# Part of the first layer's output projection into its attention, one table of score halves for both layers, and a last projection chunk by chunk

## The chip, the core and the metric

The kernel runs on 1 core of one Trainium2 chip. The metric is the device time of one execution in microseconds (us); lower is better. Three runs of the kernel before gave 2385.03, 2386.05 and 2387.29 us, median 2386.05. The engines are TensorE (PE in the profile; its weight loads are PEld), VectorE (DVE), ScalarE (ACT), GpSimd (POOL) and SyncE (SP), which issues nearly all DMAs here.

## What is computed

Two layers of a hybrid mixer over 1280 tokens: 1024 latent tokens (`NL`) and 256 context tokens (`NP`). They are the columns, and 1024 features are 8 tiles of 128 partitions. One layer, cut to what matters:

```
h = rmsnorm(x) * (1 + scale) + shift              # modulation of the layer
q, k, v, g_attn, hyena parts, lru parts = h @ w_in
y_attn = softmax(q k^T / 8) v                     # 8 heads, latent tokens also see 512 cached keys
y_hy   = x0 * long_conv(x1 * hv, filter)          # by FFT
y_lru  = rg_lru forward + backward                # the recurrent branch
mix = concat(y_attn * silu(g_attn), y_hy * silu(g_hy), y_lru * silu(g_lru))    # 12 tiles of 128 rows
x_new = x + gate * (mix @ w_out)                  # the output projection
```

After the second layer comes a final rmsnorm. Every operand of a matmul is split into two float16 halves, `hi` (rounded) and `lo` (the rest), and three products are added (hi hi, hi lo, lo hi), so one 128-row tile of a projection costs 3 matmuls for each chunk of columns. The chunks are `CH`: 512, 512 and 256 columns.

## The kernel before

**Order of a layer.** The input projections run tile by tile, with the recurrent branch and the FFT work woven between them; the gated hyena and recurrent outputs are split into halves and parked in DRAM (`park`, tensor `Md`, 8 tiles: 0 to 3 hyena, 4 to 7 recurrent). Then comes `attention`, then `outproj`. In the first layer `weave` lets two side streams run along with `outproj`: the filter spectra of the second layer (`fs`) and its modulation (`mod`, which is `ada_pairs`: 48 blocks of `w_ada` of 256 KB, each loaded, split by ScalarE and VectorE, and used by a pair of small matmuls, L505 and L506). The buffers of `ada_pairs` are the four of tag `bn`. The scheduler of the framework sets the final order of each engine's instructions from the order of emission.

**Attention.** There are 40 units (4 head pairs, 5 blocks of 256 queries, 2 heads). For each, `scores` makes the scores of 2 key tiles at a time in PSUM (L1201, L1202), takes the exponential on ScalarE, and splits it: `SPLIT` says for each of the 6 steps of a unit who makes `hi` (A: ScalarE, from PSUM once more; V: VectorE, a cast; G: GpSimd) and who subtracts for `lo` (V or G). The first layer had a table of its own, with a second row for the last head pair; per latent unit of the first three pairs it gives ScalarE 4 of 6 `hi`, VectorE 1 and GpSimd 1, and of the last pair ScalarE 1 and VectorE 5. The second layer's gives ScalarE all 6, and VectorE 2 of 6 subtractions. Between the score steps, `tick` runs the maxima of the next pairs (L1174 on TensorE, reduced at L1175 on VectorE). `values` multiplies with v (L1228, L1229), `emit_out` transposes (L1240) and gates.

**The output projection** adds, per output tile d and chunk, 12 mixer tiles in PSUM (`out_acc`, L1321), then `stt(x, acc, gt_t, xi)` on VectorE makes gate times acc plus the residual xi, which was loaded, and `Squares` gathers the squares for the next norm. The second layer (`l in SOON`) did a part of it early: `soon` is a side stream of `attention`; 24 steps, each of which loads xi, adds the 8 parked tiles (24 matmuls), applies gate and residual and stores the partial sum to `Xp` in DRAM. From unit 4 on, 0.71 steps go with each unit. Its `outproj` then adds only the four attention tiles to what it loads from `Xp`. For this the parked tiles are read back (`fetch`) ahead of the attention; in the first layer this came after it.

**End.** `outproj` takes the output tiles one by one, all three chunks of each, and only the last `LAST` = 2 together, chunk by chunk; behind a chunk's last tile come its norm (`rstd`) and `through`, which in the second layer scales and stores the result. The weights are split by `split_w` (L157 on ScalarE, L151 on VectorE) and held by `Weights` in 10 slots; a weight tile of 512 columns takes one.

## Time and profile before

| | |
|---|---|
| three runs, median | 2386.05 us (2385.03 to 2387.29) |
| the profiled execution | 2387.67 us, of which the span is 2385.9 |
| TensorE busy | 2107.8 us, 88% of the span, mean granted clock 0.959 |
| VectorE, ScalarE, GpSimd busy | 1812.1, 1226.4, 835.3 us (76, 51, 35%) |
| DMA | 215.62 MB, mean 90 GB/s |

The profile is of one execution. Shares of the span are means over stages with different limits, so the stages are read one by one. The span begins at 0; the first attention lies at 811 to 1095 us, the first output projection at 1095 to 1349, the second attention at 1973 to 2315 and the second projection with the end at 2315 to 2386. TensorE's clock stands as the share of full speed that was granted.

### The profile page before, as it was taken

How to read it: one execution, taken by the hardware profiler on the slowest of the kernel's cores; microseconds unless marked ns; L12 is line 12 of the kernel's file. 1: busy time of each engine (PE TensorE's matmuls, PEld its weight loads, DVE VectorE, ACT ScalarE, POOL GpSimd, SP SyncE). 2: the span in 40 equal slices, each digit the busy share in tenths (PEclk: the TensorE clock that was granted, in tenths of full speed). 3: DMA queues.
4: the chain of work that ended last, by engine and by line, in shares of the span. 5: the costliest groups of instructions: out<-in, count | busy, mean ns of one | idle time of the engine just before them, and what ended most of it. 6: DMA issues, size and time to landing. Idle time of an engine off the chain costs nothing. (4 is left out here: it accounts for less than half of the span.)

```text
span 2385.9 us, 38028 instructions
## 1 busy us (share of the span) xinstructions
PE 2107.8 (88%) x14288; PEld 1246.9 (52%) x14288; DVE 1812.1 (76%) x2888; ACT 1226.4 (51%) x2132; POOL 835.3 (35%) x762
## 2 busy tenths in 40 slices
PE   8777868989998888879998898999899898999996
PEld 2334434555555566665444444455555555666663
DVE  6987888487669899986868776766774998767546
ACT  6765754334333466654353577644333326656662
POOL 4442252124312467852202221131340316445440
PEclk9889989999999999979999999999999999999998
DMA  7315224134214410003563213122422334112114
GB/s 265 121 42 127 59 67 128 57 110 135 79 57 132 150 48 2 7 1 116 158 195 123 93 31 55 51 74 78 141 85 71 107 103 145 54 58 60 41 51 139
DMA packets 147786, 215.62 MB, mean 90 GB/s; under 512 B 21381, under 2 KB 71726, under 8 KB 147601
## 3 DMA queue, kind: packets, MB, share of 16 engines
q1 hardware_dynamic: 147600, 213.18, 30.0%
q8 instruction: 112, 1.84, 0.3%
q14 instruction: 74, 0.60, 0.1%
HBM read 165.49 MB, written 43.79 MB: 88 GB/s over the span
## 5 line engine op out<-in xcount | busy, mean ns | idle before, releaser
L685 PE MATMUL acc<-h,wh 128*128 128x512 f16 (+1 forms) x3264 | 865.1, 351 | 34.6 <-DVE f L151 14.3
L685 PE MATMUL acc<-h,wl 128*128 128x512 f16 (+1 forms) x1632 | 572.5, 351 | 0.0
L685 PEld LDWEIGHTS <-wh 128*128 128x128 f16 x3264 | 324.4, 100 | 319.8 <-issue 74.8
L154 POOL TENSOR_TENSOR y<-by,y 128x512 f16<-128x512 f32 x264 | 319.7, 1227 | 211.1 <-issue 93.7
L685 PEld LDWEIGHTS <-wl 128*128 128x128 f16 x1632 | 162.5, 100 | 160.5 <-issue 34.4
L157 ACT ACTIVATE f<-acc 128x512 f32<-128x512 f32 (+1 forms) x204 | 105.0, 519 | 248.6 <-PE acc L685 247.2
L157 ACT ACTIVATE by<-s 128x512 f32<-128x512 f32 x208 | 131.1, 631 | 154.4 <-PE s L1202 140.4
L1321 PE MATMUL acc<-h,wh 128*128 128x512 f16 (+1 forms) x768 | 203.6, 348 | 0.0
L151 DVE SCALAR_TENSOR_TENSOR a<-f,pr,a 128x1024 f32<-128x1024 f32 (+1 forms) x144 | 147.9, 1047 | 60.2 <-ACT a L157 57.4
L1175 DVE TENSOR_REDUCE mxl<-m 128x1 f32<-128x512 f32 x288 | 188.0, 680 | 7.2 <-PE m L1174 7.0
L1228 PE MATMUL o<-va,y 128*128 128x130 f16 x1600 | 166.8, 224 | 2.0 <-DVE f L151 1.6
L1229 PE MATMUL o<-va,y 128*128 128x65 f16 x1600 | 161.6, 195 | 5.1 <-POOL y L154 4.7
L154 DVE TENSOR_TENSOR y<-by,y 128x512 f16<-128x512 f32 x136 | 137.1, 1017 | 34.6 <-ACT y L157 34.2
L1229 PEld LDWEIGHTS <-y 128*128 128x128 f16 x1600 | 144.7, 99 | 34.0 <-issue 18.4
L157 ACT ACTIVATE wh<-wr 128x512 f16<-128x512 f32 x184 | 113.5, 625 | 93.8 <-PE acc L685 55.7
L1321 PEld LDWEIGHTS <-wh 128*128 128x128 f16 x1152 | 109.7, 98 | 95.0 <-issue 19.5
L1228 PEld LDWEIGHTS <-y 128*128 128x128 f16 x1600 | 146.6, 99 | 21.0 <-issue 14.4
L372 PE MATMUL m<-y,ld 128*128 128x256 f16 x960 | 127.4, 279 | 28.2 <-ACT y L157 10.8
L1174 PE MATMUL m<-k,a 128*128 128x512 f16 x288 | 110.7, 387 | 37.3 <-DVE mxl L1175 35.8
L154 DVE TENSOR_TENSOR y<-y,y 128x256 f32<-128x256 f32 (+4 forms) x160 | 129.8, 841 | 13.8 <-ACT y L157 13.7
L151 DVE SCALAR_TENSOR_TENSOR wl<-wr,wh 128x512 f16<-128x512 f32 x168 | 129.8, 785 | 11.4 <-ACT wh L157 10.4
L1321 PE MATMUL acc<-h,wl 128*128 128x512 f16 (+1 forms) x384 | 133.6, 348 | 0.0
(217 smaller groups left out, 4233.1 us busy)
## 6 DMA issues: line engine op xcount, KB each, us to landing
wr<-in_w_in SPq DMA_DIRECT2D x136, 256.0 KB
bn<-in_w_ada SPq DMA_DIRECT2D x64, 256.0 KB
wr<-in_w_out SPq DMA_DIRECT2D x48, 256.0 KB
ld<-in_fhl SPq DMA_DIRECT2D x56, 192.0 KB
h<-Md SPq DMA_DIRECT2D x16, 640.0 KB
h<-in_w_ada SPq DMA_DIRECT2D x16, 512.0 KB
Md<-ba SPq DMA_DIRECT2D x32, 256.0 KB
Hl<-by SPq DMA_DIRECT2D x32, 256.0 KB
```

The lines of the kernel that those rows point to most:

```text
L151: return (eng or V).scalar_tensor_tensor(out, a, s, b, o0, o1)
L154: (eng or V).tensor_tensor(out, a, b, op)
L157: A.activation(out, a, f, bias=bias, scale=scale)
L372: PE.matmul(x[:, o], cn[:, y, c], hl[:, z, g], start=(k == 0 and j == 0), stop=(k == 1 and j == 2))
L685: PE.matmul(acc[:, :n], w[k // 4][wi][:, P * (k % 4):P * (k % 4) + P], h[k][:, x, c0:c0 + n], start=(k == 0 and j == 0), stop=(k == KT - 1 ...
L1174: PE.matmul(p, lhs, k1[g][:, 512 * c:512 * c + 512], start=True, stop=True)
L1175: V.tensor_reduce(mxl[:, 8 * e + qt, c:c + 1], p, AX.X, MAX)
L1228: PE.matmul(o[:, qt], p[:, 0], va[g][:, s0 + s], start=(s == 0), stop=False)
L1229: PE.matmul(o[:, qt, 0], p[:, 1], va[g][:, s0 + s, 0], start=False, stop=(s == ns - 1))
L1321: PE.matmul(acc[:, :n], wt[:, cs], mix[k][:, x, c0:c0 + n], start=(i == 0 and j == 0), stop=(i == len(ks) - 1 and j == 2))
```

## The change

Three things are changed. (1) The side stream `soon` now runs in the first layer too, but over the four recurrent tiles alone (group 2 of the mixer tiles; `SOON` names for each layer the groups that go early): 24 steps of 12 matmuls. Weight tiles of a projection are now `u` (early) and `r` (rest) in both layers. The first `outproj` adds the other 8 tiles to the partial sums that it loads from `Xp`, and `fetch` comes ahead of the attention. (2) The second layer's row of `SPLIT` serves both layers. (3) `LAST` becomes 8 for the second layer: all its output tiles go chunk by chunk.

```diff
-N_G, LAST = (4, 4), 2
+N_G, LAST = (4, 4), (2, 8)
...
-SOON, SOON_RATE, SOON_FROM = (1,), 0.71, 4
-
-SPLIT = (("AG", "VV", "AG", "AV", "GG", "AG"), ("VG", "VG", "VV", "VV", "VV", "AG")), \
-    (("AG", "AG", "AV", "AG", "AG", "AV"), ("AG", "AG", "AV", "AG", "AG", "AV"))
+SOON, SOON_RATE, SOON_FROM = ((2,), (1, 2)), 0.71, 4
+
+SPLIT = "AG", "AG", "AV", "AG", "AG", "AV"
...
+    def groups(l, part):
+
+        return [i for i in (1, 2, 0) if (i in SOON[l]) == (part == "u")]
+
+    def tiles_of(l, part):
+        return [4 * i + j for i in groups(l, part) for j in range(4)]
...
-            how = SPLIT[l][last][s2 // 2]
+            how = SPLIT[s2 // 2]
...
-                acc = out_acc(w, [None] * 4 + parked, range(4, NMIX), c0, n)
+                acc = out_acc(w, [None] * 4 + parked, tiles_of(l, "u"), c0, n)
...
-        for ds in [(d,) for d in range(KT - LAST)] + [tuple(range(KT - LAST, KT))]:
+        for ds in [(d,) for d in range(KT - LAST[l])] + [tuple(range(KT - LAST[l], KT))]:
...
-                    xi = B("ld" if l in SOON else "ba")[:, :n]
-                    load(xi, (Xp if l in SOON else xT if l == 0 else Xs)[d, :, c0:c0 + n])
-                    acc = out_acc(w, mix, range(4) if l in SOON else [*range(4, NMIX), *range(4)], c0, n)
+                    xi = B("ld" if l else "ba")[:, :n]
+                    load(xi, Xp[d, :, c0:c0 + n])
+                    acc = out_acc(w, mix, tiles_of(l, "r"), c0, n)
...
-        if l in SOON:
-            drain(fill)
-            fetch()
-            mix = attention(l, h, st, gates, fill, EVERY[l], soon(l, parked))
-        else:
-            mix = attention(l, h, st, gates, fill, EVERY[l])
-            fetch()
-            mix += parked
+        drain(fill)
+        fetch()
+        mix = attention(l, h, st, gates, fill, EVERY[l], soon(l, parked)) + parked
```

The lines of the changed kernel are 1 lower above its new functions and 3 higher below them (L154 becomes L153, L1175 becomes L1178).

How this moves the instructions is seen best at three places, all on VectorE. The first is in the middle of the first attention (`mxl` are the maxima, `y` the halves of the exponentials, `by` the exponentials, `ba` the outputs, `ld` the stream's residual). Before:

```order
L1175 TENSOR_REDUCE mxl_7163<-m_8037 128x1
L154 TENSOR_TENSOR ba_7704<-ba_7704,o_7973 128x2x64
L1175 TENSOR_REDUCE mxl_7163<-m_8049 128x1
L154 TENSOR_TENSOR ba_7704<-ba_7704,ri_8022 128x2x64
L1214 CAST y_8032<-by_8045 128x512
L1175 TENSOR_REDUCE mxl_7163<-m_8062 128x1
L154 TENSOR_TENSOR y_8032<-by_8045,y_8032 128x512
L154 TENSOR_TENSOR y_8057<-by_8070,y_8057 128x512
```

And in the change:

```order
L1178 TENSOR_REDUCE mxl_7185<-m_8155 128x1
L1188 TENSOR_REDUCE mm_7186<-mxl_7185 128x16
L153 TENSOR_TENSOR y_8138<-by_8151,y_8138 128x512
L1235 RECIPROCAL ri_8207<-o_8158 128x2
L1236 COPY ba_8028<-o_8158 128x2x64
L153 TENSOR_TENSOR ba_8028<-ba_8028,o_8158 128x2x64
L153 TENSOR_TENSOR ba_8028<-ba_8028,ri_8207 128x2x64
L150 SCALAR_TENSOR_TENSOR f_6348<-o_8212,f_6348 128x256
L150 SCALAR_TENSOR_TENSOR ld_8218<-acc_8220,gt_t,ld_8218 128x256
```

The casts are gone, and the gated additions of the stream (`ld<-acc,gt_t,ld`) have come in; on TensorE 288 matmuls of the projection stand between the scores, in 24 groups of 12.

The second place is late in the first output projection, where the last of the modulation's six tables is copied out of PSUM (`bn<-s`). Before, 14 of the projection's 24 accumulations stand ahead of it:

```order
L151 SCALAR_TENSOR_TENSOR bn_12785<-bn_12784,bn_12785 128x512
L154 TENSOR_TENSOR by_11591<-by_11591,bn_12832 128x512
L510 TENSOR_SCALAR bn_12881<-s_12734 4x512
L154 TENSOR_TENSOR by_11592<-by_11592,bn_12931 128x512
L154 TENSOR_TENSOR modv<-s_12883,pr 128x8
L154 TENSOR_TENSOR by_11593<-by_11593,bn_13063 128x256
```

In the change 20 of 24 do; `a_13818` belongs to the last two output tiles:

```order
L150 SCALAR_TENSOR_TENSOR a_13818<-acc_13896,gt_t,ba_13894 128x512
L150 SCALAR_TENSOR_TENSOR bn_13121<-bn_13120,bn_13121 128x512
L153 TENSOR_TENSOR by_12053<-by_12053,bn_13156 128x512
L150 SCALAR_TENSOR_TENSOR y_13561<-y_13560,y_13304 128x256
L509 TENSOR_SCALAR bn_13205<-s_13070 4x512
L153 TENSOR_TENSOR by_12054<-by_12054,bn_13243 128x512
```

So the modulation's work now reaches nearly to the end of the projection's. Behind its last pair TensorE has 72 matmuls of the projection and 96 of the spectra, which stand in one block between the last two accumulations.

The third place is the end of the second projection (`fin_t` marks the final scaling, `acc` an accumulation). Before, the first chunk's scaling stands behind all long accumulations:

```order
L151 SCALAR_TENSOR_TENSOR a_25205<-acc_25275,gt_t,ld_25273 128x512
L154 TENSOR_TENSOR bn_25249<-bn_25249,bn_25247 128x512
L151 SCALAR_TENSOR_TENSOR a_25204<-acc_25320,gt_t,ld_25318 128x256
L151 SCALAR_TENSOR_TENSOR bn_25246<-bn_25249,bn_25247 128x512
L154 TENSOR_TENSOR by_24860<-by_24860,bn_25270 128x512
L151 SCALAR_TENSOR_TENSOR f_24862<-f_24862,fin_t,bn_25246 128x512
```

In the change it stands between those of the second chunk:

```order
L150 SCALAR_TENSOR_TENSOR bn_25142<-bn_25145,bn_25143 128x512
L153 TENSOR_TENSOR by_24980<-by_24980,bn_25183 128x512
L150 SCALAR_TENSOR_TENSOR f_24982<-f_24982,fin_t,bn_25142 128x512
L150 SCALAR_TENSOR_TENSOR f_24984<-acc_25188,gt_t,ld_25186 128x512
L150 SCALAR_TENSOR_TENSOR f_24983<-f_24983,fin_t,bn_25142 128x512
L150 SCALAR_TENSOR_TENSOR f_24984<-f_24984,fin_t,bn_25142 128x512
```

The 8 accumulations of the third chunk (256 columns), which before stood tile by tile among the others, now stand together at the end.

## Rows read from the trace of the kernel before

**Rows 1.** The page, part 1: busy time, share of the span, instructions.

```profile
PE 2107.8 (88%) x14288; PEld 1246.9 (52%) x14288; DVE 1812.1 (76%) x2888; ACT 1226.4 (51%) x2132; POOL 835.3 (35%) x762
```

**Rows 2.** Windows of three stages: us; PE, PEld, DVE, ACT, POOL busy; PEclk; DMA share, GB/s.

```profile
811.00:1095.00 284.00, 232.19 (x2621) 181.58 (x2619) 259.35 (x482) 167.29 (x334) 200.46 (x177) 0.93 0.12 37
1095.00:1349.00 254.00, 237.03 (x1298) 118.70 (x1298) 182.66 (x279) 114.17 (x195) 39.44 (x23) 0.98 0.49 154
1973.00:2315.00 342.00, 318.96 (x3204) 227.50 (x3202) 232.73 (x450) 219.96 (x443) 179.95 (x161) 0.99 0.22 67
```

**Rows 3.** Groups, first attention, PE: count | busy us, mean ns | idle before, releaser.

```profile
L1174 PE MATMUL m<-k,a 128*128 128x512 f16 x144 | 55.1, 387 | 27.1 <-DVE mxl L1175 26.4
```

**Rows 4.** Groups, second attention, PE.

```profile
L1321 PE MATMUL acc<-h,wh 128*128 128x512 f16 (+1 forms) x384 | 98.8, 343 | 0.0
...
L1321 PE MATMUL acc<-h,wl 128*128 128x512 f16 (+1 forms) x192 | 66.0, 344 | 0.0
L1174 PE MATMUL m<-k,a 128*128 128x512 f16 x144 | 55.6, 386 | 10.2 <-DVE mxl L1175 9.4
```

**Rows 5.** Groups, first attention, DVE: subtractions and casts.

```profile
L154 DVE TENSOR_TENSOR y<-by,y 128x512 f16<-128x512 f32 x72 | 75.9, 1071 | 0.3
L1214 DVE CAST y<-by 128x512 f16<-128x512 f32 x66 | 50.2, 781 | 4.3 <-ACT by L157 4.3
```

**Rows 6.** Groups, second attention, DVE: subtractions, the stream's additions, weight splits.

```profile
L154 DVE TENSOR_TENSOR y<-by,y 128x512 f16<-128x512 f32 x64 | 61.2, 957 | 34.3 <-ACT y L157 34.2
...
L151 DVE SCALAR_TENSOR_TENSOR ld<-acc,gt_t,ld 128x512 f32<-128x512 f32 (+1 forms) x24 | 15.9, 661 | 48.0 <-PE acc L1321 47.7
...
L151 DVE SCALAR_TENSOR_TENSOR wl<-wr,wh 128x512 f16<-128x512 f32 x16 | 11.0, 686 | 2.1 <-ACT wh L157 1.7
```

**Rows 7.** Groups, second attention, ACT: a rounded half from PSUM.

```profile
L157 ACT ACTIVATE y<-s 128x512 f16<-128x512 f32 x104 | 67.2, 646 | 0.0
```

**Rows 8.** Timeline, PE, end of the second projection: start us, us, instruction.

```profile
2357.07 0.38 PE L1321 MATMUL acc<-a,wl 128*128 128x512 f16 x1
...
2359.66 0.38 PE L1321 MATMUL acc<-a,wl 128*128 128x512 f16 x1
2359.87 0.38 PE L1321 MATMUL acc<-a,wh 128*128 128x256 f16 x2
2360.09 0.27 PE L1321 MATMUL acc<-a,wl 128*128 128x256 f16 x1
```

**Rows 9.** Windows: last head pair of the second attention and of the first.

```profile
2240.00:2315.00 75.00, 72.12 (x783) 54.21 (x780) 35.28 (x75) 53.55 (x109) 43.35 (x40) 1.00 0.14 44
1023.00:1095.00 72.00, 58.80 (x633) 47.67 (x632) 64.47 (x115) 33.07 (x63) 38.29 (x32) 0.80 0.03 9
```

**Rows 10.** Line L1321, second attention: ns min/median/max, first and last start.

```profile
L1321 PEld LDWEIGHTS <-wh x407: 95/98/98, 2014.0 to 2314.6; 128*128 128x128 f16 x136
```

**Rows 11.** Groups, first projection, DVE: weight splits.

```profile
L151 DVE SCALAR_TENSOR_TENSOR wl<-wr,wh 128x512 f16<-128x512 f32 x21 | 18.7, 900 | 0.3 <-PE acc L1321 0.2
```

**Rows 12.** Line L506, first projection: the second matmul of each modulation pair.

```profile
L506 PE MATMUL s<-bn,silu_p x48: 376/377/584, 1098.3 to 1274.4; 128*2 128x512 f16 x48
```

**Rows 13.** Waits, first projection: us in total, times, longest us.

```profile
ACT bn L157 <- DMA bn<-in_w_ada: 39.9, 23, 6.3
...
PE s L506 <- DVE bn L151: 7.7, 6, 3.8
```

**Rows 14.** Window from TensorE's last matmul of the projection to the end.

```profile
2362.40:2386.00 23.60, 2.60 (x7) 0.80 (x4) 19.30 (x33) 4.08 (x8) 2.83 (x3) 0.58 0.61 223
```

**Rows 15.** Timeline, DVE, the end: scaling, accumulation and addition of squares.

```profile
2363.15 0.74 DVE L151 SCALAR_TENSOR_TENSOR f<-f,fin_t,bn 128x512 f32<-128x512 f32 x1
2363.82 0.68 DVE L154 TENSOR_TENSOR by<-by,bn 128x512 f32<-128x512 f32 x1
...
2371.20 0.48 DVE L151 SCALAR_TENSOR_TENSOR a<-acc,gt_t,ld 128x256 f32<-128x256 f32 x1
...
2372.25 0.42 DVE L154 TENSOR_TENSOR by<-by,bn 128x256 f32<-128x256 f32 x1
```

More of the change, by code (lines that the diff above doesn't have):

```diff
@@ L647, in __init__ @@
                 names += [f"ga{i}" for i in range(4)]
-                names += [f"{x}{d}" for x in "ur" for d in range(KT)] if l in SOON else list(range(KT))
+                names += [f"{x}{d}" for x in "ur" for d in range(KT)]
                 self.todo += [(l, n) for n in names]
@@ L654, in pull @@
                 l, n = self.todo[0]
-                size = 3 if isinstance(n, int) else 1 if n[0] == "r" else 2
+                size = len(groups(l, n[0])) if n[0] in "ur" else 2
                 if need not in self.done and need is not None:
@@ L661, in pull @@
                 self.live.append(((l, n), size))
-                if isinstance(n, int):
-                    v = [split_w(w_out[l, n, :, 512 * i:512 * i + 512], WENG["o"]) for i in (1, 2, 0)]
-                elif n[0] in "ur":
-                    v = [split_w(w_out[l, int(n[1]), :, 512 * i:512 * i + 512], WENG["o"])
-                         for i in ((1, 2) if n[0] == "u" else (0,))]
+                if n[0] in "ur":
+                    v = [split_w(w_out[l, int(n[1]), :, 512 * i:512 * i + 512], WENG["o"]) for i in groups(l, n[0])]
                 else:
@@ L1190, in q_finish, with scores @@
         return mt
-    def scores(l, st, e, c0, last, tick):
+    def scores(st, e, c0, tick):
         g, q1, q2 = st
@@ L1295, in attention @@
                 next(mx)
-            pts = scores(l, st[pair], e, c0, pair == 3, tick if pair < 3 else lambda: None)
+            pts = scores(st[pair], e, c0, tick if pair < 3 else lambda: None)
             if e == 0:
@@ L1348, in outproj @@
                 for d in ds:
-                    name = f"r{d}" if l in SOON else d
+                    name = f"r{d}"
                     w = W.get(l, name)
-                    xi = B("ld" if l in SOON else "ba")[:, :n]
-                    load(xi, (Xp if l in SOON else xT if l == 0 else Xs)[d, :, c0:c0 + n])
-                    acc = out_acc(w, mix, range(4) if l in SOON else [*range(4, NMIX), *range(4)], c0, n)
+                    xi = B("ld" if l else "ba")[:, :n]
+                    load(xi, Xp[d, :, c0:c0 + n])
+                    acc = out_acc(w, mix, tiles_of(l, "r"), c0, n)
                     if c0 == NL:
```

## The prediction, on record before the run

> **What bounds the kernel now.** The page's first part comes first: TensorE is busy for 88% of the span [rows 1], so no stage can shrink much unless TensorE's work there moves or its waits go. The next view is the table of windows, one for each stage that the change touches [rows 2]: the first attention (811 to 1095 us, 284), the first output projection (1095 to 1349, 254), the second attention (1973 to 2315, 342). The reader is to see that they have different limits. In the first attention VectorE is busy for 259 of 284 us, TensorE for 232, at a granted clock of 0.93 (the mean of its two levels, 1.2 and 2.4 GHz). In the second it is the other way round: TensorE 319 of 342, VectorE 233, clock 0.99. In the first projection TensorE has 237 of 254.
>
> The groups by engine say why. In the first attention TensorE waits 26.4 us for the reduction of the maxima, which is VectorE's [rows 3]. In the second the same wait is 9.4 us, and the 576 matmuls of the side stream (384 and 192) waited for nothing [rows 4]. So the second attention is a stage on TensorE's own pace, and the first one is VectorE's.
>
> **The change, part by part.**
>
> *First attention.* It loses work on VectorE: the 66 casts, 50.2 us, go, and 72 subtractions become 64 [rows 5]; at the second attention's durations those take 61.2 us [rows 6], 14.7 less. It gains the 24 gated additions of the stream, 15.9 us, and 8 weight splits at 686 ns, 5.5 us [rows 6]. Net 50.2 + 14.7 - 15.9 - 5.5 = 43.5 us less on VectorE. ScalarE makes the rounded halves instead: by the two tables 110 before and 200 now, 90 more at about 646 ns [rows 7], overlapped in its pipeline; the second attention carries all 200 and ScalarE is busy there for 220 us [rows 2]. GpSimd loses 24 casts and gains 8 subtractions.
>
> It gains work on TensorE: 24 steps of 12 matmuls, 192 of 512 columns and 96 of 256. What one costs is the distance between starts in an unbroken run: 12 of 512 columns in 2.59 us, so 0.216, and two of 256 in 0.22 [rows 8]; I use 0.109 for one of those. This is 192 x 0.216 + 96 x 0.109 = 51.9 us.
>
> The stage after the change is the second attention with half of its stream: same table, same tick rate, 24 steps of 12 matmuls and not 24. That row is the nearest, so I take 342 - 51.9 = 290, or **+6 us** against 284. Bounds: above, nothing of the shorter steps is won, 342 (+58); below, the 23 us in which TensorE idles in the second attention vanish too, 267 (-17). The last quarter speaks for a value near 290 and not above: it takes 72 us now, VectorE busy for 64 of them and the clock at 0.80, and 75 us in the second attention at clock 1.00, TensorE 72 [rows 9]. With less stream there ScalarE, 54 of 75, still has room.
>
> The transfers move with the steps. SP now issues, inside the attention, 24 loads of the input, 24 stores of the partial sums and 8 weight loads, and ahead of it the 8 reloads of the parked halves; the loads of the next pair's queries stand behind stores that wait for VectorE. The cover is the one of the second attention, where all this is done already: its stream began 41 us after the stage [rows 10], and that delay is inside the 342. DMA's share in the first attention is 0.12 [rows 2], so there is room. If the cover failed, the next pair's first scores would wait.
>
> *First output projection.* It loses the same 288 matmuls, 51.9 us, and 8 of its 24 weight splits, about 7.2 us of VectorE at 900 ns [rows 11]. Its loads come from the partial sums and not from the input, same size, stored long before. Three readings of what is left: TensorE, if its pauses stay, 254 - 51.9 = 202. VectorE, if it keeps its share of 183 in 254: (183 - 7)/0.72 = 244. And the modulation stream of the second layer: its 48 matmul pairs ran from 1098.3 to 1274.4 us, one each 3.7 us [rows 12], each behind a 256 KB load that ScalarE waited for 23 times [rows 13]. The order of the change keeps these pairs in the stage almost to its end (the last table stands behind 20 of 24 accumulations, not 14), so it cannot be shorter than about 3 + 176 + 21 = 200, where 21 us is what TensorE's order leaves behind the last pair: 24 long and 48 short matmuls of the projection and a block of 96 short ones of the spectra (5.2 + 5.2 + 10.5 at the distances above). That block is fed by VectorE and ScalarE two tiles at a time and will not run unbroken. I take 210, near the two readings that agree plus some 8 us for the block: **-44 us**.
>
> Here the trace is to be weighed against a rule. The stage's weight loads are busy for 119 of 254 us, 47%, its matmuls for 237 [rows 2]. The Trainium skill (Perfetto Trace Analysis, Identifying the Most-Contended Engine) says that matmul busy time misjudges how near TensorE is to its limit and that the busy share of LDWEIGHTS is to be read instead. By that rule TensorE has half the stage free, and the projection would hang on VectorE, as in rival C. The trace speaks against it for this shape: a 512-column matmul holds the array for 0.216 us, and its weight load takes 0.098 [rows 10], so the share could not pass 45% with the array full. By that rule the time would be 2377 us, by the row 2343.
>
> *Second layer.* Its score table had this content already: 0. Its projection goes chunk by chunk over all 8 tiles: the 8 weights fit (1 slot each of 10) and were all loaded before. The last 512-column matmul ends 6 x 12 x 0.109 = 7.8 us earlier, since the 256-column ones of six tiles now come behind it. After TensorE's last matmul the end took 23.6 us, VectorE busy for 19.3 [rows 14]: the final scaling of two chunks, 0.67 us from one start to the next, among it [rows 15]. Of this the first chunk's 8, 5.4 us, now stand among the second chunk's accumulations; added behind the last long matmul are 6 additions and 6 accumulations of 0.42 and 0.48 us, 5.4 us. That is 7.8 + 5.4 - 5.4 = 7.8; chains of small steps will take some back: **-5 us**, between 0 and -9.
>
> *Sum.* +6 - 44 - 5 = -43. The profiled execution took 2387.67 us (span 2385.9, 1.8 around it), so it would be 2344.7; the median of the three runs is 1.6 lower, so **2343 us**.
>
> **The rivals.**
>
> *B, the stream fits into the attention's holes.* VectorE's 43.5 us and the clock are won, TensorE runs without pauses: 267, and 202 for the projection: -17 - 52 - 5 = -74, 2312 us. For it: the first attention ran at 0.93. Against: no stretch of this kernel with scores in it runs without pauses.
>
> *C, the projection is held by its side streams.* It stays at VectorE's 72%, 244 us: +6 - 10 - 5 = -9, 2377. For it: 39.9 us of waits for the modulation's loads, and TensorE's 7.7 us for its halves [rows 13], which get closer together. Against: those visible waits of TensorE are small beside 254.
>
> *D, slower: a step costs the same whatever its length.* The price of a step of the stream would be the accumulator that it takes from the scores (two buffers, shared), its wait in VectorE's queue and its two transfers on SP, not its matmuls. The first attention then takes the second's 342: +58 - 44 - 5 = +9, 2395. It decides from (44 + 5)/24 = 2.0 us per step, beside 2.2 us of matmuls. Against: in the second attention the stream's matmuls waited 0.0 us [rows 4].
>
> That the change doesn't do what it says is excluded by the order: 288 matmuls stand between the scores.
>
> **How the numbers follow.** The forecast has a chance of 0.58 (its own range 2326 to 2362: the attention from -2 to +16, the projection from -55 to -34, the end 0 to -9). B has 0.16, C 0.19, D 0.07. A range from 2313 to 2378 leaves out the lower half of B, something like half of C and all of D, about 2 in 10. A measurement of this kernel tells 0.2% from no change, 4.8 us. Faster by more: the forecast, B and most of C (0.58 + 0.16 + 0.14 = 0.88). Within: the rest of C, 0.05. Slower: D, 0.07.
>
> **What would show it.** In the profile after: a first attention of 285 to 298 us with TensorE above 92%, VectorE below 85%, a clock of 0.98 or more, and no casts; a projection of 200 to 220 us with TensorE still near 90%; from the last 512-column matmul to the end some 28 us. Wrong would be: waits of the scores for query loads (D's place), TensorE in the projection waiting for the modulation's halves for tens of us (C), or a first attention under 275 (B).

## The result, and the profile after

The changed kernel takes **2354.43 us** (median of 4 runs, 2349.57 to 2357.53) against 2386.67 for the kernel before (median of 4 runs): a ratio of 0.987, 95% interval 0.9856 to 0.9885, 32 us less. The forecast was 2343 us, 11 us lower. The profiled execution of the change is the fastest of its four (2349.57 us, span 2347.8), so its stages add up to a gain of 38 us, and the median to 32.

The windows of the four stages after, in the columns of [rows 2], the end as the fourth:

```profile
809.10:1097.40 288.30, 264.25 (x2911) 197.57 (x2910) 225.39 (x443) 213.83 (x434) 179.91 (x161) 1.00 0.25 78
1097.40:1317.90 220.50, 190.43 (x1005) 92.17 (x1003) 173.66 (x266) 102.24 (x175) 36.91 (x21) 0.94 0.53 171
1944.00:2286.30 342.30, 319.43 (x3205) 227.64 (x3203) 232.65 (x452) 220.55 (x443) 179.78 (x161) 0.99 0.22 68
2286.30:2347.80 61.50, 48.38 (x265) 25.92 (x262) 44.18 (x74) 18.30 (x33) 3.36 (x4) 0.92 0.47 150
```

The first attention has turned into a smaller second one, as the forecast wanted: TensorE 264 of 288 us, VectorE down from 259 to 225, clock 1.00. The first projection is the row to look at: it lost 33 us, and TensorE's busy time in it 47 (237 to 190), so that TensorE now stands still for 30 of 220 us, where it did for 17 of 254 [rows 2].

From here on the stages are cut at their first and last matmuls, by the same rule in every kernel (first score matmul of the stage, last transpose, first input-projection matmul of the second layer). One profile of each:

| kernel | up to it | first attention | first projection | second layer's rest | second attention | end | span |
|---|---|---|---|---|---|---|---|
| before | 811.1 | 284.3 | 253.4 | 623.9 | 342.7 | 70.5 | 2385.9 |
| after | 809.1 | 288.2 | 220.5 | 626.1 | 342.3 | 61.5 | 2347.8 |
| difference | -2.0 | +3.9 | -32.9 | +2.2 | -0.4 | -9.0 | -38.1 |

Stages that no edit touches differ by up to some 5 us from kernel to kernel (623.9 to 629.3 for the second layer's rest), so less than that is not read as an effect.

### The profile page after: what moved, and what is told of

Read it like the earlier page. It is cut to its first block, busy times and chain, and to the rows that moved or that the text cites. A ratio compares the mean times of both kernels' runs of the same rounds, so it can differ in the third digit from the quotient of the medians.

```text
span 2347.8 us, 38185 instructions
## 1 busy us (share of the span) xinstructions
PE 2095.4 (89%) x14288; PEld 1236.4 (53%) x14288; DVE 1771.4 (75%) x2838; ACT 1266.3 (54%) x2222; POOL 810.3 (35%) x746
## 5 line engine op out<-in xcount | busy, mean ns | idle before, releaser
L153 POOL TENSOR_TENSOR y<-by,y 128x512 f16<-128x512 f32 x272 | 317.0, 1184 | 230.1 <-issue 139.2
L156 ACT ACTIVATE by<-s 128x512 f32<-128x512 f32 x208 | 136.0, 654 | 110.2 <-PE s L1205 109.5
L1178 DVE TENSOR_REDUCE mxl<-m 128x1 f32<-128x512 f32 x288 | 186.2, 681 | 8.8 <-PE m L1177 8.8
L153 DVE TENSOR_TENSOR y<-by,y 128x512 f16<-128x512 f32 x128 | 120.7, 943 | 68.2 <-ACT y L156 66.8
L1232 PE MATMUL o<-va,y 128*128 128x65 f16 x1600 | 155.2, 193 | 8.4 <-POOL y L153 7.3
L1231 PE MATMUL o<-va,y 128*128 128x130 f16 x1600 | 160.3, 220 | 1.7 <-DVE f L150 1.6
L371 PE MATMUL m<-y,ld 128*128 128x256 f16 x960 | 129.4, 282 | 31.9 <-ACT y L156 14.0
L1232 PEld LDWEIGHTS <-y 128*128 128x128 f16 x1600 | 140.7, 98 | 24.7 <-POOL y L153 9.3
L1231 PEld LDWEIGHTS <-y 128*128 128x128 f16 x1600 | 142.0, 97 | 12.6 <-issue 7.8
L156 ACT ACTIVATE y<-s 128x512 f16<-128x512 f32 x208 | 137.0, 659 | 0.0
L153 DVE TENSOR_TENSOR y<-y,y 128x256 f32<-128x256 f32 (+4 forms) x160 | 129.9, 840 | 8.6 <-ACT y L156 8.5
```

The costliest lines, as they stand in the source:

```text
L153: (eng or V).tensor_tensor(out, a, b, op)
L156: A.activation(out, a, f, bias=bias, scale=scale)
L371: PE.matmul(x[:, o], cn[:, y, c], hl[:, z, g], start=(k == 0 and j == 0), stop=(k == 1 and j == 2))
L1178: V.tensor_reduce(mxl[:, 8 * e + qt, c:c + 1], p, AX.X, MAX)
L1231: PE.matmul(o[:, qt], p[:, 0], va[g][:, s0 + s], start=(s == 0), stop=False)
L1232: PE.matmul(o[:, qt, 0], p[:, 1], va[g][:, s0 + s, 0], start=False, stop=(s == ns - 1))
```

## The experiments

Two theories stood at the beginning. The forecast's own was this: the stream carries matmuls from a stage that TensorE fills into one that has room after VectorE is relieved, so stream and table belong together. The rival was this: the table of halves earns the gain, and the stream only moves time from one stage to the next.

### One part alone: the table

```diff
-SPLIT = (("AG", "VV", "AG", "AV", "GG", "AG"), ("VG", "VG", "VV", "VV", "VV", "AG")), \
-    (("AG", "AG", "AV", "AG", "AG", "AV"), ("AG", "AG", "AV", "AG", "AG", "AV"))
+SPLIT = ((("AG", "AG", "AV", "AG", "AG", "AV"),) * 2,) * 2
```

> The kernel before with one change only: the second layer's table of halves in the first attention too. If the first attention was held by VectorE (my theory), its work falls from 259 to about 204 us and the stage becomes the second attention without any stream: 342 - 24 x 24 matmuls (103.8) = 238, so 238 to 252 us in place of 284, and the whole 2341 to 2354. If ScalarE or the chain of a unit holds it (rival), it stays above 270 us and the whole above 2372. If the table is worth 35 us or more alone, the stream itself has brought next to nothing in the changed kernel.

Measured: 2353.61 us (2350.38 to 2360.53), ratio 0.987 (0.985 to 0.9889): the same ratio as the whole change, from one part of it. Windows of this kernel, first attention and first projection:

```profile
809.10:1064.80 255.70, 225.51 (x2625) 173.57 (x2624) 204.24 (x409) 207.23 (x424) 181.81 (x161) 0.97 0.13 41
1064.80:1319.50 254.70, 237.53 (x1291) 118.45 (x1289) 182.53 (x279) 113.85 (x194) 39.16 (x23) 0.97 0.48 154
```

VectorE goes from 259 to 204 us in the attention, and the stage follows by 28.6; the projection is what it was. TensorE's wait for VectorE's reductions of the maxima, 26.4 us before [rows 3], is 14.4 here, and the wait of its transposes for VectorE's outputs (`ba`) falls from 15.1 to 2.5 us. The two differences add up to 24.6 of the 28.6 us. Groups here, then the waits for `ba` before and here:

```profile
L1174 PE MATMUL m<-k,a 128*128 128x512 f16 x144 | 54.5, 385 | 15.8 <-DVE mxl L1175 14.4 <-DVE mm L1181 0.5
```

```profile
PE o L1240 <- DVE ba L154: 15.1, 6, 4.1
```

```profile
PE o L1240 <- DVE ba L154: 2.5, 4, 1.0
```

### One part alone: the end

```diff
-N_G, LAST = (4, 4), 2
+N_G, LAST = (4, 4), (2, 8)
...
-        for ds in [(d,) for d in range(KT - LAST)] + [tuple(range(KT - LAST, KT))]:
+        for ds in [(d,) for d in range(KT - LAST[l])] + [tuple(range(KT - LAST[l], KT))]:
```

> The kernel before with one change only: the second layer's last projection chunk by chunk over all 8 tiles. My theory: the end (from the second attention's last output to the end of the span, 70.5 us before) takes 61.5 us as in the changed kernel, so 9 us less, 2377. Rival: part of the 9 us came from the rest of the change, and this one alone brings 5 us, 2381.

Measured: 2375.1 us (10 runs), ratio 0.9961 (0.995 to 0.9972); the end takes 61.8 us and not 70.5. That is 9 us, in the place where it was forecast:

```profile
2317.60:2379.40 61.80, 48.45 (x265) 25.98 (x263) 44.24 (x74) 18.30 (x33) 3.36 (x4) 0.92 0.45 149
```

### Twice the stream

```diff
-SOON, SOON_RATE, SOON_FROM = ((2,), (1, 2)), 0.71, 4
+SOON, SOON_RATE, SOON_FROM = ((1, 2), (1, 2)), 0.71, 4
```

> The changed kernel with the first layer's stream over hyena and recurrent tiles (24 steps of 24 matmuls, as in the second layer). The first attention: priced by matmul it grows by 51.9 us to 340; priced by step (rival) it stays at 288. The first projection, 220 us in the changed kernel, loses another 288 matmuls: if TensorE held it, it falls by 52 to 168; if the chain of the second layer's modulation holds it (48 pairs at 3.7 us, my theory now), it stays at 205 to 225, and the whole becomes 2390 to 2405.

Measured: 2394.5 us, ratio 1.0049 (1.0032 to 1.0067). Windows, first attention and first projection:

```profile
806.20:1145.20 339.00, 317.75 (x3203) 226.95 (x3201) 231.85 (x453) 221.00 (x445) 178.48 (x161) 0.99 0.23 74
1145.20:1363.10 217.90, 143.39 (x714) 67.81 (x713) 168.46 (x258) 96.93 (x166) 36.73 (x21) 0.80 0.51 163
```

With the kernel that has the table and no stream in this layer, this gives the account of the stream by stages, from one profile each. 288 matmuls cost 52 us at the distances of [rows 8]:

| matmuls moved | first attention | first projection | both |
|---|---|---|---|
| 0 (table alone) | 255.7 | 254.7 | 510.4 |
| 288 (the change) | 288.2 (+32.5) | 220.5 (-34.2) | 508.7 |
| 576 (twice) | 339.0 (+50.8) | 217.9 (-2.6) | 556.9 |

The first 288 cost the attention 32.5 us, 19 less than their price. Of this, 6 us are places where TensorE had stood still (30.2 us without the stream, 24.1 with it). The granted clock went from 0.97 to 1.00 as well: by the mean, TensorE spent some 15 us of the stage without the stream at the lower of its two levels, and none with it, which is worth about 8 us (an estimate from the two clocks); the rest was not separated. The second 288 cost nearly their full price, although TensorE still stood still for 24 us before them. In the projection the first 288 give back 34 of 52 us and the second almost nothing. So the rule "a step costs its matmuls" holds (24 steps of 12 more matmuls: 2.1 us a step more), and rival D falls. But **the stream nets nothing** in these two stages: what it saves in one it costs in the other.

### Table and end, without the stream

The table's edit and the end's edit above, both on the kernel before.

> The kernel before with the second layer's table of halves in the first attention and with the end of the second layer chunk by chunk, but with no side stream in the first layer (its projection does all twelve tiles). Theory 'the stream nets nothing': the two savings seen apart add, 2386 - 28 - 9 to 10 = 2346 to 2352 us, within 0.3% of the whole change; first attention 256, first projection 254, end 61.5 us. Rival 'the stream is what pays once the table is there': this is slower than the whole change by 1% or more, over 2375 us.

Measured: **2345.31 us** (2343.12 to 2347.54), ratio 0.9826 (0.981 to 0.9842). This beats the change: its interval lies under the change's 0.9856 to 0.9885. Windows:

```profile
808.00:1063.90 255.90, 225.75 (x2625) 173.66 (x2624) 204.18 (x409) 207.33 (x424) 181.92 (x161) 0.97 0.13 41
1063.90:1317.10 253.20, 235.20 (x1292) 117.67 (x1290) 183.56 (x279) 113.83 (x194) 38.92 (x23) 0.99 0.47 154
```

The two stages take 509.1 us, and 508.7 in the change. The medians are 9 us apart, the profiled spans 2.8 (2345.0 and 2347.8; the change's profile is of its fastest run). So the times show that the stream costs some us on top of the table, and the profiles do not show where.

### The stream with the old table

```diff
-SPLIT = "AG", "AG", "AV", "AG", "AG", "AV"
+SPLIT = (("AG", "VV", "AG", "AV", "GG", "AG"), ("VG", "VG", "VV", "VV", "VV", "AG")), \
+    (("AG", "AG", "AV", "AG", "AG", "AV"), ("AG", "AG", "AV", "AG", "AG", "AV"))
...
-            how = SPLIT[s2 // 2]
+            how = SPLIT[l][last][s2 // 2]
...
```

> The changed kernel with the table of halves that the first layer had before; side stream and chunked end stay. If the table's gain stands by itself, the first attention is longer than the change's 288 by what the table alone gave, 28 us: 317, the whole 2381 to 2385. Rival 'the side stream fills the waits that the old table leaves' (27 us of waits for emission's halves in the first attention before): the first attention is 290 to 303 and the whole 2357 to 2369, that is, table and stream gain the same time and the gains do not add.

(The 27 us of this text are the waits of [rows 3], which are for the maxima and not for halves of the emission.)

Measured: 2391.67 us, ratio 1.0045 (1.003 to 1.006). The first attention takes 325.2 us, more than either theory said; the projection 222.6. The rival (the stream fills the old table's waits) falls clearly, and the gains do not simply add either: with the stream the table is worth 37 us, without it 28.6. Window and waits of TensorE in this first attention:

```profile
809.60:1134.80 325.20, 276.72 (x2910) 202.95 (x2907) 278.74 (x516) 172.91 (x344) 201.81 (x177) 0.96 0.21 69
```

```profile
PE m L1178 <- DVE mxl L1179: 24.2, 38, 2.2
PE o L1244 <- DVE ba L154: 15.8, 4, 4.1
```

The wait for the maxima is nearly the 26.4 us of [rows 3]: the stream's matmuls did not fill it, since VectorE has its 24 additions to do as well and is busy for 279 us. The reading is that on a stage that VectorE sets, the stream is paid on two engines.

With this run all four combinations of table and stream are measured, each with the chunked end (ratio to the kernel before):

| | old table | new table |
|---|---|---|
| no stream | 0.9961 | 0.9826 |
| stream | 1.0045 | 0.987 |

The table gains 1.35% (32 us) without the stream and 1.75% (42 us) with it. The stream costs 0.84% (20 us) with the old table and 0.44% (10 us) with the new one. In this respect the forecast's theory was right: the stream does better with the table. But it does not pay even there, and the table does not need the stream.

### Why the projection gave back 34 us and not 52

Groups of TensorE in the first projection, those with idle time ahead of them (count | busy us, mean ns | idle before, releasers). Before:

```profile
L372 PE MATMUL m<-y,ld 128*128 128x256 f16 x240 | 31.8, 278 | 3.2 <-ACT y L157 3.2
L505 PE MATMUL s<-bn,silu_p 128*4 128x512 f16 x48 | 18.3, 382 | 3.3 <-ACT bn L157 3.2
L506 PE MATMUL s<-bn,silu_p 128*2 128x512 f16 x48 | 18.3, 381 | 7.7 <-DVE bn L151 7.7
...
L420 PE MATMUL m<-y,ones 128*128 128x256 f32 x8 | 2.7, 418 | 1.0 <-POOL y L154 0.9
```

After:

```profile
L1324 PE MATMUL acc<-h,wh 128*128 128x512 f16 x120 | 38.8, 388 | 0.4 <-DVE f L150 0.4
L371 PE MATMUL m<-y,ld 128*128 128x256 f16 x240 | 33.4, 288 | 7.4 <-ACT y L156 3.9 <-DVE y L153 1.9 <-DMA ld<-in_fhl 1.4
...
L504 PE MATMUL s<-bn,silu_p 128*4 128x512 f16 x48 | 18.7, 390 | 2.1 <-ACT bn L156 2.1
L505 PE MATMUL s<-bn,silu_p 128*2 128x512 f16 x48 | 18.1, 377 | 11.7 <-DVE bn L150 11.7
L1324 PE MATMUL acc<-h,wh 128*128 128x256 f16 x64 | 12.6, 285 | 1.2 <-DVE f L150 1.2
...
L569 PE MATMUL m<-by,ones 128*128 128x512 f32 x4 | 3.1, 867 | 5.7 <-DVE by L153 5.7
```

Added up, TensorE waits 15.2 us before and 28.5 after: 4 more for the low halves of the modulation's weights (L505), 4.2 more inside the spectra (L371), 5.7 ahead of the norm's sums (L569). The reading is that the work behind these waits was there all along and that the 288 matmuls had stood in front of them. The waits are 13 of the missing 18 us. The rest goes with matmuls that took longer (a spectra matmul 288 ns and not 278), at a mean granted clock of 0.94 and not 0.98; it was not separated further.

The modulation's 48 pairs, first to last start, before [rows 12] and after:

```profile
L505 PE MATMUL s<-bn,silu_p x48: 375/377/379, 1097.5 to 1278.2; 128*2 128x512 f16 x48
```

The 48 pairs took 176.1 us before and 180.7 after (176.5 with the table alone, 183.1 with twice the stream), whatever stood between them. This looked like a chain that sets the stage: 181 us of pairs and 39.7 behind. The next runs went to that theory.

**More buffers.**

```diff
-BUFS = {"h": 8, "f": 4, "a": 8, "y": 8, "by": 6, "ld": 4, "bn": 4, "ba": 3, "wr": 4, "wh": 10, "acc": 2, "s": 2, "o": 2, "m": 2}
+BUFS = {"h": 8, "f": 4, "a": 8, "y": 8, "by": 6, "ld": 4, "bn": 5, "ba": 3, "wr": 3, "wh": 10, "acc": 2, "s": 2, "o": 2, "m": 2}
```

> The changed kernel with five buffers of tag bn and not four (and three raw weight buffers and not four, for the space). If the modulation's chain is held by its buffers (a load waits until VectorE has read the block two before it), the 48 pairs come faster than the 181 us that they take in the changed kernel, 150 to 170, and the projection falls from 220 to 195 to 212 us. If it is held by what stands between on TensorE or VectorE, the pairs stay at 175 to 185 us and the time within 5 us of the changed kernel; three raw weight buffers may cost some us elsewhere.

Measured: 2359.95 us, ratio 0.9895 (0.9873 to 0.9917); pairs 182.9 us, projection 224.1. One buffer more, with one raw weight buffer less, does nothing for the pairs; more was not tried.

```profile
L505 PE MATMUL s<-bn,silu_p x48: 376/377/586, 1104.4 to 1287.3; 128*2 128x512 f16 x48
```

**No modulation.**

```diff
+    def no_mod():
+        V.memset(modv[:, 1], 0.5)
+        ada_in(1)
+        V.tensor_scalar(gt_t[:, 1], modv[:, 1, 16:24], 1.0 / SW, None, MUL)
+        yield
...
-        mod = ada_pairs(1) if l == 0 else iter(())
+        mod = no_mod() if l == 0 else iter(())
```

> The changed kernel without the second layer's modulation in the first projection (its values are a constant; the 48 pairs of matmuls, their loads, copies and subtractions are left out). Theory 'the chain of 48 modulation pairs sets the first projection after the change': the projection falls from 220 us to what its matmuls take, 8 x 40 projection matmuls at 0.216 us (69 us) and filter work beside them, to at most 180 us, the whole to 2315 us or less. Rival 'the filter spectra set it' (their side work on VectorE and ScalarE and the block of 96 at the end): it stays at 205 us or more, the whole at 2338 us or more.

**Half of its loads.**

```diff
-                raw, w = B("bn"), B("bn", (P, 2, 512), F16)
-                load(raw, w_ada[l, k, :, P * o:P * o + 512])
+                if l == 0 or k % 2 == 0:
+                    raw = B("bn")
+                    load(raw, w_ada[l, k, :, P * o:P * o + 512])
+                w = B("bn", (P, 2, 512), F16)
```

> The changed kernel in which the second layer's modulation loads every second 256 KB block only, and each block serves two pairs (half of the weights are left out); copies, subtractions and matmuls of all 48 pairs stay. Theory 'the loads set the chain's 3.8 us a pair' (their issue in SP's queue behind other waits, or their transfer): pairs first to last falls from 181 us to 150 or less, the projection to 195 us or less. Rival 'VectorE's queue sets it' (73 to 78% busy in this stretch, the subtraction of each pair in order behind the side work): first to last stays at 170 us or more and the projection at 212 or more.

**No low halves.**

```diff
+                if l:
+                    PE.matmul(p[:4], silu_p[:, k], w[:, 0], start=(k == 0), stop=(k == KT - 1))
+                    if k % 4 == 3:
+                        yield
+                    continue
                 if AE[k % 2] == "G":
```

> The changed kernel in which the second layer's modulation is made from the high halves alone: the 48 subtractions on VectorE and 48 of its 96 matmuls are left out; all 48 loads and copies stay. Theory 'VectorE's queue sets the chain': pairs first to last falls from 181 us by the 48 subtractions' own 48 x 0.69 = 33 us at the least, to 148 us or less. Rival 'the loads set it': it stays at 165 us or more, and the projection at 205 us or more.

Measured: 2308.77, 2342.37 and 2325.66 us (2 runs each); ratios 0.9675, 0.9816 and 0.9746. The window of the projection without modulation:

```profile
1092.20:1275.90 183.70, 152.27 (x885) 90.73 (x884) 141.60 (x201) 76.23 (x131) 38.83 (x21) 0.92 0.44 143
```

With half of its loads, the pairs, and the windows up to the last pair and behind it:

```profile
L507 PE MATMUL s<-bn,silu_p x48: 376/377/631, 1096.2 to 1220.7; 128*2 128x512 f16 x48
```

```profile
1096.10:1220.70 124.60, 113.57 (x597) 50.86 (x596) 103.13 (x162) 62.97 (x112) 18.44 (x11) 0.99 0.50 162
1220.70:1307.80 87.10, 69.36 (x409) 42.18 (x408) 72.87 (x106) 38.40 (x65) 18.23 (x10) 0.90 0.42 137
```

And without low halves:

```profile
L500 PE MATMUL s<-bn,silu_p x48: 376/377/506, 1100.2 to 1275.9; 128*4 128x512 f16 x48
```

```profile
1100.20:1293.80 193.60, 166.84 (x957) 89.60 (x957) 141.51 (x221) 99.49 (x174) 39.34 (x21) 0.97 0.60 196
```

These three took the theory of the chain down, and each broke an expectation: without modulation the projection takes 183.7 us, a little over the 180 of the theory; the other two meet neither theory nor rival in full. Half of the loads makes the pairs run in 124.5 us and not 181: so the loads set the pace of the pairs. (With them go 24 of the turns in the ring of `bn`; that the fifth buffer did nothing speaks against the ring as the cause.) But the projection loses only 9 us (211.7), because 87 us of other work now come behind the last pair, with VectorE busy for 73 of them. Without the low halves it is the reverse: the pairs still take 176 us, and the projection loses 27 (193.6), with 18 us behind the last pair and not 40. So **the pairs' pace does not set the stage**: speeding it up by 56 us is worth 9. What went with the low halves is 48 matmuls of 512 columns (10 us at 0.216) and 32 us of VectorE's work (173.7 to 141.5); the 27 us are more than the matmuls, so VectorE's work carries part of the stage too. Without any modulation 37 us go.

Where VectorE is late can be seen at the largest wait. TensorE, VectorE and GpSimd around it in the changed kernel (start us, us, instruction, idle before):

```profile
1260.57 0.38 PE L1324 MATMUL acc<-h,wh 128*128 128x512 f16 x1
1264.68 0.38 PE L505 MATMUL s<-bn,silu_p 128*2 128x512 f16 x1 [3.73 <-DVE bn L150]
```

```profile
1258.51 3.37 DVE L153 TENSOR_TENSOR y<-y,ld 128x1024 f32<-128x1024 f32 x1
1261.80 2.82 DVE L150 SCALAR_TENSOR_TENSOR bn<-bn,bn 128x512 f16<-128x512 f32 x1
```

```profile
1258.13 5.95 POOL L153 TENSOR_TENSOR y<-y,ld 128x1024 f32<-128x1024 f32 x2 [2.63 <-DVE ld L424]
```

The low half takes 2.82 us where the line's median is 0.685:

```profile
L150 DVE SCALAR_TENSOR_TENSOR bn<-bn,bn x46: 616/685/2825, 1098.6 to 1312.6; 128x512 f16<-128x512 f32 x45, 128x512 f32<-128x512 f32 x1
```

It starts under GpSimd's multiplication of the filter by its norm, which ends at 1264.08 us (1258.13 + 5.95), and ends 0.54 us behind it. Over the stage, of the 61 low halves (`bn` and `wl`) the 45 during which GpSimd did nothing took at most 0.694 us, and the 16 that overlap with an instruction of GpSimd 1.46 on average, up to 2.83: 12 us more than 16 usual ones. What tells the 16 apart is which came first: the nine that started while GpSimd's instruction ran all ended 0.54 to 0.55 us behind its end, and the seven that had started before it took at most 0.69 us. Five of the eight waits for L505's halves, 9.8 of the 11.7 us, come right behind such a long half (at 1134.7, 1139.6, 1144.4, 1155.0 and 1264.7 us), each under one of GpSimd's ten operations on 128x1024. The Trainium skill (GPSIMD Engine Reference, Specifications) says that GpSimd shares its interfaces to SBUF with VectorE and contends with VectorE's instructions that have two inputs in SBUF; the trace agrees for these halves, which have. Over all VectorE instructions on 512 SBUF columns and more, those that overlap with GpSimd's take 16.4 us longer in this stage before, and 16.7 after, than as many of the same shape that do not. So the loss is not new; more of it now reaches TensorE, whose waits for these halves went from 7.7 to 11.7 us. No run moved GpSimd's ten operations away, so what that would bring stays open.

Each of these four kernels leaves TensorE 27 to 31 us short of the stage's length (220.5 less 190.4, 183.7 less 152.3, 211.7 less 182.9, 193.6 less 166.8). A reading that fits these four, and is not shown: TensorE works through its list in order, the list is its work plus the waits at the points where VectorE's and ScalarE's products are due, and these waits hardly shrink when something is taken out. It does not cover all: with twice the stream TensorE falls short by 74 us (217.9 less 143.4), at a clock of 0.80. What sets the 218 us there, where pairs (183 us) and VectorE (168) both lie near, was not separated. Nor was it tried whether the loads' pace comes from SP's queue, where they stand behind other waits, or from the transfers.

### Two tries to repair the projection

Every second low half of the modulation on GpSimd:

```diff
-AE = "VV"
+AE = "VG"
```

> The changed kernel in which the low half of every second block of the modulation's weights (both layers) is made on GpSimd, by two operations, in place of VectorE's one. Theory 'the subtractions in VectorE's queue hold the pairs': 24 of 48 leave VectorE in the first projection, so that it falls by about half of what leaving out all 48 gave (27 us), to 203 to 210 us, the whole to 2335 to 2343. Rival 'GpSimd's two operations (1.9 and 1.3 us in its rows) make the block later than VectorE's 0.9 did': the projection stays at 218 us or more, and the 176 to 181 us of the pairs grow; the first layer's own modulation at the start can lose too, start over 809.

Measured: 2372.98 us (10 runs), ratio 0.9957 (0.9941 to 0.9972): the rival. Pairs and waits of TensorE in the projection, and GpSimd's two groups:

```profile
L505 PE MATMUL s<-bn,silu_p x48: 376/377/586, 1107.1 to 1305.4; 128*2 128x512 f16 x48
```

```profile
PE s L505 <- POOL bn L153: 17.3, 14, 3.9
```

```profile
L153 POOL TENSOR_TENSOR bn<-bn,bn 128x512 f16<-128x512 f32 x23 | 30.5, 1327 | 1.8
L500 POOL TENSOR_SCALAR bn<-bn 128x512 f32<-128x512 f32 x23 | 22.1, 959 | 89.6 <-ACT bn L156 77.4 <-PE s L505 6.6 <-PE acc L1324 5.3
```

A half now takes 0.96 + 1.33 = 2.3 us on GpSimd, where it took some 0.9 on VectorE; TensorE waits 17.3 us for them, and the projection takes 231.5. The part before the first attention, which has the first layer's own modulation, grew as well (818.7 us). VectorE was rid of 23 halves, but its busy time in the stage fell by 4.4 us alone (169.3 against 173.7), and the halves it kept took 1.0 us on average, up to 2.84, where they had taken 0.9: with more work on GpSimd, VectorE's instructions took longer.

The spectra spread over the stage:

```diff
-R_FS1 = 3.466
+R_FS1 = 6.0
```

> The changed kernel with the rate of the second layer's filter spectra in the first projection raised from 3.466 to 6.0, so that the 96 spectra matmuls, which now stand together behind the last modulation pair, are spread over the stage, and projection matmuls alone end it. Theory 'the block at the end waits for ScalarE and VectorE with nothing beside it' (7 us within it, 6 us before the norm): these waits go, the projection falls by 5 to 13 us to 207 to 215, the whole to 2341 to 2349. Rival 'the stage is set by VectorE's sum of work (174 us of 220) and the wait only moves': within 4 us of 220, with new waits before the modulation pairs.

Measured: 2345.45 us (2344.11 to 2348.93), ratio 0.9856 (0.9839 to 0.9874); projection 215.9, 4.6 less, between the two theories. In the waits of TensorE those ahead of the norm (5.7 us) are gone, while those for the modulation's high halves rose from 2.1 to 5.0:

```profile
PE s L505 <- DVE bn L150: 12.4, 7, 3.7
PE m L371 <- ACT y L156: 7.1, 4, 2.5
PE s L504 <- ACT bn L156: 5.0, 6, 1.7
```

Its interval overlaps the change's, so a gain over the change is likely but not shown.

On top of that, the low halves of the projection's own weights on GpSimd:

```diff
-R_FS1 = 3.466
+R_FS1 = 6.0
...
-                    v = [split_w(w_out[l, int(n[1]), :, 512 * i:512 * i + 512], WENG["o"]) for i in groups(l, n[0])]
+                    v = [split_w(w_out[l, int(n[1]), :, 512 * i:512 * i + 512], "G" if (l, n[0]) == (0, "r") else WENG["o"]) for i in groups(l, n[0])]
```

> A try at a version that beats both: the changed kernel with the rate of the filter spectra at 6.0, and with the low halves of the eight weight tiles of the first layer's output projection that are left to it made on GpSimd (37 of 220 us busy there), not on VectorE. Theory 'the waits behind VectorE are the projection's loss': VectorE is rid of 8 x 0.85 = 7 us, the projection falls from 216 to 208 to 213 us and the whole to 2337 to 2343, under the 2345 of the kernel with the table and the chunked end alone. Rival 'GpSimd's two operations make weights late, as they made the modulation's': projection at 218 us or more, the whole over 2347.

Measured: 2354.43 us (2353.16 to 2355.65), ratio 0.9878 (0.9859 to 0.9897): 9 us over the median with the spread spectra alone (the intervals of the two ratios overlap by a little), projection 220.9. TensorE waits for no weight of GpSimd's by name, but VectorE's busy time did not fall either (172.5 against 172.1 us). Six of the eight halves were made within the stage, and VectorE spent 4.7 us less on `wl` there; against that stand four scalings of the next norm that now fall into the stage (3.0 us) and other instructions that took longer. The time that VectorE's instructions lose under GpSimd's, counted as above, is 16 us with and without this edit, so it is not that which grew. The fastest kernel of all that compute the whole thing stays the one with table and end alone, level with the spread spectra.

## Why the prediction was right, and where it was wrong

The total came within the forecast's range, and each stage moved the way that was said. But the credit was given wrongly: the forecast has the stream's matmuls as the gain, and without the stream the time is 2345 us, nearer to the forecast than the change itself. That the total is near is in part luck: the projection gave 11 us less than forecast, attention and end 6 more.

- **First attention, +6: measured +3.9.** The way it was made, the second attention less half of its stream, is confirmed by the kernel with twice the stream: 339.0 us, near the second attention's 342, and 50.8 more than the change. TensorE's 92%, VectorE's 78% and the clock of 1.00 came as said, and the casts are gone. What the term hid is its make-up: -28.6 by the table and +32.5 by the stream. The forecast costed 43.5 us less on VectorE and 51.9 more on TensorE and never asked what the first was worth alone; that question would have shown that the table carries the gain. Its price of a cast (50.2 us for 66) was in part waiting behind GpSimd, as the last section shows.
- **First projection, -44: measured -32.9.** This is the term that was mis-sized, and its failed step is "three readings of what is left", of which two agreed near 200. The first, TensorE with its pauses as they were (202), failed because the pauses grew: 28.5 us of waits and not 15.2. The third, 176 us of pairs and 21 behind, failed in its tail: the pairs kept their pace (180.7), but 39.7 us came behind them, where the forecast had 21 and 8 for the spectra. They held 5.7 us for the norm, which it had not priced, and waits inside the spectra. The second, VectorE's share (244), took its busy time as its own work, while some 16 us of it are waits behind GpSimd. So the two readings agreed near 200 by chance, and neither was a bound that holds the other work.
- **End, -5: measured -9.0**, at the edge of its bounds. The step "chains of small steps will take some back" was wrong: the last long matmul starts 8.4 us sooner after the second attention (7.8 were worked out), and from there to the last instruction it takes 25.6 us, 26.2 before. Nothing was taken back. The last long matmul after, to be laid beside [rows 8]:

```profile
2322.15 0.38 PE L1324 MATMUL acc<-a,wl 128*128 128x512 f16 x1
```

- **Sum, -43: measured -38.1 in the profiles and -32 in the medians.** Stages that no term covers add nothing (-2.0 and +2.2). The remaining 6 us are the change's own spread, whose profile is its fastest run.
- **Rival B** (the stream fits into holes) is partly true: the stream cost 19 us less than its matmuls, 6 of them from TensorE's standing still and about 8 from the clock. But that is against a stage of 256 us and not of 284, so it did not show in the total. **Rival C** named the right place and the right engines: TensorE's waits for the modulation's halves went from 7.7 [rows 13] to 11.7 us. Its price was too high, since VectorE's share of the stage rose from 72 to 79%. **Rival D** fell with the run of twice the stream.
- **The rule on weight loads.** In the projection before, weight loads were busy for 47% and matmuls for 93% of the stage [rows 2]; 288 matmuls out gave 34 of their 52 us, so TensorE had held two thirds of it, and 2354 lies nearer to the row's 2343 than to the 2377 by the rule of the Trainium skill (Perfetto Trace Analysis, Identifying the Most-Contended Engine). Where the next 288 went out, from a stage with 42% and 86%, only 2.6 us came back; there the warning of the Trainium skill (same section) that matmul busy time is no good measure of how near TensorE is to its limit agrees with the trace. The busy share of weight loads, 47% and then 42%, does not tell the two stages apart either. And the 45% that the forecast worked out as the ceiling holds for 512-column matmuls alone: about half of this stage's matmuls have 256 columns and start every 0.109 us [rows 8], and its share, 47%, is over that ceiling already.

## What to carry to other kernels

When two parts of a change meet in one stage, price each alone too: here the table had the gain and the stream a small loss, which the sum could not tell. Work moved between stages gains only what it fills in the new place less the waits it uncovers in the old one, so list the waits that it stood in front of. A chain of even pace is not thereby the stage's bound (halve it, and see whether the stage follows), and where an instruction's mean lies well above its median, look for the engine that blocks it before work is moved there.

## What was not expected of the hardware

A VectorE subtraction of 0.685 us took up to 2.83 us while GpSimd worked on large operands in SBUF. The means of 0.90 us in [rows 11] and of 0.69 in [rows 6] for the same instruction are this: a mix of 0.68 and of up to 2.8, and not two prices. The same stands behind [rows 5]. In the first attention before, 38 of the 66 casts started under an instruction of GpSimd and took 1.05 us on average, where the other 28 took 0.42; of the 72 subtractions 47 took 1.28 us so, where the others took 0.68:

```profile
L154 DVE TENSOR_TENSOR y<-by,y x72: 674/1078/1698, 819.9 to 1082.8; 128x512 f16<-128x512 f32 x72
L1214 DVE CAST y<-by x66: 412/740/1403, 818.5 to 1085.2; 128x512 f16<-128x512 f32 x66
```

Over all shapes, VectorE's instructions that started under one of GpSimd's took 59 us longer there than as many of the same shape that did not, and 30 us with the table alone. So about half of the 55 us that the table took off VectorE in this stage (259 to 204) was waiting behind GpSimd, and not VectorE's own work; that the forecast could not see in means.

So idle time on GpSimd (37 busy of 220 us) is not free to use: giving it 46 operations more made VectorE's rest slower, and a low half, 0.96 + 1.33 us there, later.
